# Low parts of the keys made by POOL from a ScalarE copy, from the third head pair on

## The chip, the core and the metric

The kernel runs on one core of one Trainium2 chip. The metric is the device time of one execution in microseconds; lower is better. Engines are named as the profile names them: PE is TensorE, DVE is VectorE, ACT is ScalarE, POOL is GpSimd, SP issues most of the DMAs.

## The reference

One layer of a streaming encoder, batch 1, 1024 positions, model width 1024. A modulated layer norm feeds one input projection; eight heads of forgetting attention and eight of stick-breaking attention, each 64 wide, read its columns; each head's output is gated by a SiLU, and all go through one output projection into a residual and a last layer norm.

```python
u = _layer_norm(x) * (1.0 + scale) + shift
h = u @ w_in[layer]
fq, fk, fv, fg, ff, sq, sk, sv, sg = _split_columns(h)
...
# forgetting attention, per head and block of 128 queries
s = einsum('bhqd,bhkd->bhqk', q, k) * scale + (f_q[..., :, None] - f_k[..., None, :])
p = softmax(where(causal, s, -inf)); out = p @ v
...
# stick-breaking attention
z = einsum('bhqd,bhkd->bhqk', q, k) * scale
later = cumsum(log_sigmoid(-z), reverse=True) - log_sigmoid(-z)   # on the strict causal part
w = where(strict, exp(log_sigmoid(z) + later), 0); out = w @ v
...
y = concatenate([y_fox * silu(fg), y_sb * silu(sg)]) @ w_out[layer]
x = _layer_norm(alpha * x + gate * y, ln_g, ln_b)
```

## The kernel before

Products are made more exact by splitting operands into a rounded high part and a low part (the remainder) and adding several matmuls: a projection takes three matmuls for each block of 128 of the contraction (`L255`, `L256`, `L257`: high input by high weight, low by high, high by low). The weights are split by POOL: `L124` makes the high part, `L125` the low part (`L826`, `L827` do the same for the attention output read back from memory).

The sixteen heads are worked as eight pairs; a pair fills 128 partitions, head 0 in rows 0 to 63 and head 1 in rows 64 to 127. Pairs 0 to 3 are stick-breaking, 4 to 7 forgetting attention. One unit of attention is a pair, a head and a block of 128 queries. A unit's scores go into one PSUM tile `S` of 1024 columns, of which there is one buffer: `L410` multiplies keys by the queries' high and low parts, `L411` the low parts of the keys (`klo`, traced as `kl`) by the queries (`qz`, copied by ACT at `L388`). In stick-breaking units ACT reads `S` twice (`L430` into `kp`, `L431` into `be`), DVE scans `kp` (`L436`, `L440`), POOL multiplies (`L444`). In forgetting units DVE takes the row sums (`L417` into `a` and `nm`), ACT the exponential (`L423`), DVE the reciprocal, POOL the scaling (`L425`). Two units later PE transposes the weights into `T` (`L461`, two PSUM buffers), ACT copies the high part to `pt` (`L463`), DVE makes its low part (`L464`), and after every second unit PE multiplies by the values (`L476`) into `pv`. ACT copies half of `pv` into a `ty` tile (`L495`, two SBUF buffers), DVE adds (`L496`), POOL applies the gate (`L497`), and SP stores it to memory (`L505`, traced as `y_dr<-ty`).

The projections of the next pairs (`gen_m`; values by `v_tile`, `L310` to `L312`) are filled in between the matmuls of attention. Each half of 512 positions is accumulated in a PSUM tile of the tag `acc`, which has two buffers, and evicted by `evac_m`: for keys that is `evac_k`. There ACT rounds each head's rows into `kst` (`L240`, traced as `k<-m`), SP copies the rounded rows to the other half of the partitions (`L242`), and DVE subtracts the rounded values from the accumulator into `klo` (`L243`). The accumulator's buffer is free for a later projection when both subtractions are done.

PE's order is written out by hand; the orders of ACT, DVE, POOL and SP are set by a scheduler when the kernel is built, by its own estimates.

Of the kernel before, what the change touches and what calls it, by code (L numbers as in the profile page):

```python
# [8 lines left out]
F32 = mybir.dt.float32  # L9
F32R = mybir.dt.float32r  # L10
AF = mybir.ActivationFunctionType
ALU = mybir.AluOpType

P = 128
# [4 lines left out]
HD = 64  # L19
# [8 lines left out]
def tile_hybrid_layer(  # L28
# [17 lines left out]
    nc = tc.nc  # L46

    cp = ctx.enter_context(tc.tile_pool(name="const", bufs=1))
    sb = ctx.enter_context(tc.tile_pool(name="sb", bufs=1))
# [185 lines left out]
    def evac_k(p, ch, acc, kst, klo, heads):  # L235
        s = slice(ch * 512, ch * 512 + 512)
        for h in heads:
            r = slice(h * HD, h * HD + HD)
            o = slice((1 - h) * HD, (1 - h) * HD + HD)
            first = nc.scalar.copy(kst[h][r, s], acc[r, :])  # L240
            kf = kst[h].bitcast(F32)
            nc.sync.dma_start(kf[o, s], kf[r, s])  # L242
            last = nc.vector.tensor_tensor(klo[r, s], acc[r, :], kf[r, s], op=ALU.subtract)  # L243
        return first, last

    def evac_g(p, ch, acc, sg):
# [12 lines left out]
    qst, kst, klo, sgt, vt = {}, {}, {}, {}, {}  # L259
# [11 lines left out]
    def evac_m(p, m, ch, acc, heads=(0, 1)):  # L271
        if m == 0:
            evac_q(p, ch, acc, qst[p], heads)
        elif m == 1:
            return evac_k(p, ch, acc, kst[p], klo[p], heads)
        else:
            evac_g(p, ch, acc, sgt[p])
# [364 lines left out]
    for kb in range(NB):  # L642
        last = kb == NB - 1
# [95 lines left out]
    for kb in range(NB):  # L739
# [13 lines left out]
        if kb < len(evacs):  # L753
            n, h = evacs[kb]
# [209 lines left out]
    for k in range(len(units) + LAG + 1):  # L964
        if k < len(units):
# [12 lines left out]
            p, h, i = units[k]  # L978
# [86 lines left out]
```

## Time and profile before

| what | value |
|---|---|
| median of 3 runs (lowest, highest) | 690.2 us (690.01, 690.37) |
| the profiled execution's own time | 689.96 us |
| its span in the profile | 688.2 us |
| busy: PE, DVE, ACT, POOL | 98%, 66%, 56%, 62% |
| granted TensorE clock, mean | 0.998 |

The span is what the records cover; the rest of an execution's time lies around it. Rows of a group read: line, engine, operation, output and inputs, shape and count, then busy time and mean nanoseconds of one, then the idle time ahead of them and what ended it. Rows of a timeline read: start in us, duration in us, engine, line and operation; in brackets the idle time ahead and what ended it. A row with x2 stands for two like operations in a row.

### The profile page before, as it was taken

Reading aid. Unit: us, or ns where it says so; the run is one execution under the profiler, and the core shown is the slowest. Engines: PE = TensorE matmul, PEld = TensorE weight load, DVE = VectorE, ACT = ScalarE, POOL = GpSimd, SP = SyncE. Lnnn points to the kernel's source line nnn. Section 1 sums busy time; section 2 is a strip of 40 time slices with the busy share of each in tenths; the row PEclk is TensorE's granted clock in tenths of the full one; section 3 lists DMA queues with packets and bytes.
Section 4 is the critical chain, followed back from the end, with each engine's and each line's share of the span. In section 5 each row is a group of like instructions: output and inputs, shape, how many; then the busy total and the mean of one; then the engine's idle time right before and its main releaser. Section 6 shows DMA issues by size and latency. Waiting matters only on the chain.

```text
span 688.2 us, 11786 instructions
## 1 busy us (share of the span) xinstructions
PE 674.0 (98%) x4033; PEld 589.7 (86%) x4033; DVE 453.5 (66%) x924; ACT 382.1 (56%) x862; POOL 425.7 (62%) x555
## 2 busy tenths in 40 slices
PE   8999999999999999999999999999999999999996
PEld 4789898888998888889998888889988889888885
DVE  5985458767657676767675665656665767774645
ACT  5666457856657666666674564655565666531000
POOL 4567978656439565556388897877584364665411
PEclk9999999999999999999999999999999999999999
DMA  8956232112102122112144553454341288143301
GB/s 306 416 233 230 85 108 57 26 40 53 40 9 70 41 55 55 38 47 62 25 136 153 177 160 116 146 163 145 100 143 46 67 293 352 56 155 119 128 32 61
DMA packets 44028, 81.59 MB, mean 119 GB/s; under 512 B 5120, under 2 KB 18752, under 8 KB 43072
## 3 DMA queue, kind: packets, MB, share of 16 engines
q1 hardware_dynamic: 42816, 76.65, 34.0%
q10 hardware_dynamic: 1152, 4.19, 2.2%
q8 instruction: 32, 0.52, 0.3%
q14 instruction: 28, 0.23, 0.1%
HBM read 60.34 MB, written 16.29 MB: 111 GB/s over the span
## 4 chain that ended last, share of the span: by engine, by line
PE 92%; DVE 3%; DMA 2%; POOL 1%; issue 1%; ACT 0%; SPq 0%; POOLq 0%; DVEq 0%
PE m L255 10%; PE pv L476 10%; PE m L256 10%; PE m L257 10%; PE T L461 9%; PE S L411 5%; PE S L410 5%; PE o L848 4%; PE o L846 4%; PE o L847 4%; PE v L310 4%; PE v L312 4%; PE v L311 4%; DMA wss<-in_w_ss_dram 1%; DMA x<-in_x_dram 1%
## 5 line engine op out<-in xcount | busy, mean ns | idle before, releaser
L255 PE MATMUL m<-uh,whi 128*128 128x512 f32 x304 | 126.4, 416 | 0.5 <-DVE kl L243 0.5
L256 PE MATMUL m<-ul,whi 128*128 128x512 f32 x304 | 119.8, 394 | 0.0
L257 PE MATMUL m<-uh,wlo 128*128 128x512 f32 x304 | 119.6, 394 | 0.0
L464 DVE TENSOR_TENSOR pt<-T,pt 128x512 fp32r<-128x512 f32 (+2 forms) x192 | 100.5, 550 | 17.9 <-ACT pt L463 16.8
L444 POOL TENSOR_TENSOR be<-be,kp 128x127 f32<-128x127 f32 (+3 forms) x64 | 77.1, 1205 | 33.5 <-DVE kp L440 23.6
L463 ACT CAST pt<-T 128x512 fp32r<-128x512 f32 (+2 forms) x192 | 85.7, 480 | 16.7 <-PE T L461 13.0
L436 DVE TENSOR_TENSOR_SCAN kp<-kp,floor 128x512 f32<-128x512 f32 (+2 forms) x64 | 65.1, 1018 | 32.1 <-ACT kp L430 31.3
L476 PEld LDWEIGHTS pv<-pt,v 128*128 128x128 f32 (+1 forms) x640 | 77.2, 163 | 4.5 <-DVE pt L464 0.7
L476 PE MATMUL pv<-pt,v 128*128 128x256 f32 (+3 forms) x640 | 80.5, 271 | 0.5 <-DVE pt L464 0.5
L425 POOL TENSOR_SCALAR a<-a,l 128x1024 f32<-128x1024 f32 (+3 forms) x64 | 47.9, 748 | 39.5 <-DVE l L424 25.9
L423 ACT ACTIVATE a<-a,nm 128x1024 f32<-128x1024 f32 (+3 forms) x64 | 49.8, 778 | 34.0 <-DVE nm L417 33.0
L257 PEld LDWEIGHTS m<-uh,wlo 128*128 128x128 f32 x304 | 57.1, 188 | 13.5
L410 PE MATMUL S<-k,q 128*128 128x512 f32 (+5 forms) x192 | 66.5, 348 | 0.2 <-DVE nm L417 0.2
L411 PE MATMUL S<-kl,qz 128*128 128x512 f32 (+5 forms) x192 | 65.5, 342 | 0.0
L255 PEld LDWEIGHTS m<-uh,whi 128*128 128x128 f32 x304 | 57.3, 188 | 9.2 <-DVE kl L243 0.9
L256 PEld LDWEIGHTS m<-ul,whi 128*128 128x128 f32 x304 | 57.4, 189 | 8.0
L497 POOL TENSOR_TENSOR ty<-ty,sg 64x256 f32<-64x256 f32 x64 | 47.4, 741 | 24.6 <-DVE ty L496 12.2
L417 DVE CUSTOM_DVE_ANT_0 a<-S,fb 128x1024 f32<-128x1024 f32 (+3 forms) x64 | 48.3, 755 | 20.4 <-PE S L411 9.8
L430 ACT ACTIVATE kp<-S 128x128 f32<-128x128 f32 (+3 forms) x64 | 41.7, 651 | 31.8 <-PE S L411 28.3
L310 PE MATMUL v<-whi_v,uh 128*128 128x256 f32 (+1 forms) x192 | 56.0, 292 | 0.7 <-DVE kl L243 0.7
L388 ACT CAST qz<-q 64x128 fp32r<-64x128 f32 x128 | 37.4, 295 | 33.0 <-PE S L411 31.9
L312 PE MATMUL v<-wlo_v,uh 128*128 128x256 f32 (+1 forms) x192 | 54.2, 282 | 0.0
(291 smaller groups left out, 1611.5 us busy)
## 6 DMA issues: line engine op xcount, KB each, us to landing
raw<-in_w_qkg_dram SPq DMA_DIRECT2D x38, 256.0 KB, 2.8
wss<-in_w_ss_dram SPq DMA_DIRECT2D x7, 1024.0 KB, 8.3
x<-in_x_dram SPq DMA_DIRECT2D x8, 512.0 KB, 7.3
k<-k SPq DMA_DIRECT2D x32, 128.0 KB, 2.5
wg<-in_w_gate_dram SPq DMA_DIRECT2D x8, 512.0 KB, 4.4
raw_o<-in_w_out_dram SPq DMA_DIRECT2D x16, 256.0 KB, 2.7
fb<-f_dr ACTq DMA_DIRECT2D x8, 512.0 KB, 4.2
wo_dr<-whi_o SPq DMA_DIRECT2D x16, 256.0 KB, 2.5
```

The costliest lines, as they stand in the source:

```text
L255: nc.tensor.matmul(acc, hi[:, c], u_hi[kt][:, s], start=(kt == 0), stop=False)
L256: nc.tensor.matmul(acc, hi[:, c], u_lo[kt][:, s], start=False, stop=False)
L257: nc.tensor.matmul(acc, lo[:, c], u_hi[kt][:, s], start=False, stop=(kt == NB - 1))
L310: nc.tensor.matmul(acc[:, :n], u_hi[kt][:, ts_], hi[:, s], start=(kt == 0), stop=False)
L312: nc.tensor.matmul(acc[:, :n], u_hi[kt][:, ts_], lo[:, s], start=False, stop=(kt == NB - 1))
L410: nc.tensor.matmul(S[:, s, :w], qst[p][h][:, qs], kst[p][h][:, ks], start=True, stop=False)
L411: nc.tensor.matmul(S[:, s, :w], z, klo[p][:, ks], start=False, stop=True)
L436: scan = nc.vector.tensor_tensor_scan(rv, rv, floor[0][:, 512 - n:][:, ::-1], initial=0.0, op0=ALU.mult, op1=ALU.max)
L444: nc.gpsimd.tensor_tensor(be[:, :ke - 1], be[:, :ke - 1], kp[:, 1:ke], op=ALU.mult)
L463: nc.scalar.copy(hi[:, :n, qo:qo + P], t3)
L464: nc.vector.tensor_tensor(lo[:, :n, qo:qo + P], t3, hi.bitcast(F32)[:, :n, qo:qo + P], op=ALU.subtract)
L476: nc.tensor.matmul(acc[:m, q0:256], vt[p][:, kb, h * P:h * P + m], pt[:, kb % 4, q0:], start=start, stop=stop)
```

## The change

For pairs 2 to 7, in both halves, ACT copies the whole accumulator (128 by 512, unrounded) into an SBUF tile of the tag `ty` after the two casts, and POOL subtracts the rounded keys from that copy, one head's 64 rows at a time. DVE no longer takes part, and only ACT reads the accumulator. Pairs 0 and 1 stay as they were. Lines behind the edit move down by 7 in the changed kernel: its copy is `L247`, its subtraction `L250`, and a line such as `L425` is `L432` there.

```diff
             first = nc.scalar.copy(kst[h][r, s], acc[r, :])
             kf = kst[h].bitcast(F32)
             nc.sync.dma_start(kf[o, s], kf[r, s])
-            last = nc.vector.tensor_tensor(klo[r, s], acc[r, :], kf[r, s], op=ALU.subtract)
+            if p < 2:
+                last = nc.vector.tensor_tensor(klo[r, s], acc[r, :], kf[r, s], op=ALU.subtract)
+        if p >= 2:
+            whole = sb.tile([P, 512], F32, tag="ty", bufs=2, name=f"kr_{p}_{ch}")
+            nc.scalar.copy(whole, acc)
+            for h in heads:
+                r = slice(h * HD, h * HD + HD)
+                last = nc.gpsimd.tensor_tensor(klo[r, s], whole[r, :], kst[h].bitcast(F32)[r, s], op=ALU.subtract)
         return first, last
```

PE's order is the same on both sides. The scheduler gives the others new orders. ACT around the second half of pair 3's keys, while attention works on pair 2, head 1 (`kp_1_3` is head 1, block 3, with the pair left out; the number at the end of a name is a buffer), before:

```order
L463 CAST pt_2_1_0_0_3062<-T_1_0_0_3064 128x128
L240 CAST k_0_2893<-m_1_1_2996 64x512
L430 ACTIVATE kp_1_3_3083<-S_1_3_3080 128x512
L431 ACTIVATE be_1_3_3084<-S_1_3_3080 128x512
L388 CAST qz_83<-q_1_1577 64x128
L463 CAST pt_2_1_0_0_3062<-T_1_1_0_3103 128x2x128
L240 CAST k_1_2894<-m_1_1_2996 64x512
L430 ACTIVATE kp_1_4_3121<-S_1_4_3116 128x640
```

and in the changed kernel:

```order
L470 CAST pt_2_1_0_0_3068<-T_1_0_0_3070 128x128
L240 CAST k_0_2897<-m_1_1_3002 64x512
L240 CAST k_1_2898<-m_1_1_3002 64x512
L247 COPY kr_1_3084<-m_1_1_3002 128x512
L437 ACTIVATE kp_1_3_3091<-S_1_3_3088 128x512
L438 ACTIVATE be_1_3_3092<-S_1_3_3088 128x512
L395 CAST qz_83<-q_1_1577 64x128
L470 CAST pt_2_1_0_0_3068<-T_1_1_0_3111 128x2x128
```

The second cast has moved ahead of the reads of `S`, and the copy stands behind it. DVE around the second half of pair 6's keys, before:

```order
L243 TENSOR_TENSOR kl_5332<-m_1_1_5437,k_0_5330 64x512
L464 TENSOR_TENSOR pt_5_0_1_0_5472<-T_0_2_0_5518,pt_5_0_1_0_5471 128x3x128
L417 ISA a_1_7_5553,nm_1_7_5554<-S_1_7_5548,fb_5063 128x1024
L417 ISA nm_1_7_5554 128x1
L243 TENSOR_TENSOR kl_5332<-m_1_1_5437,k_1_5331 64x512
L395 TENSOR_TENSOR fb_5063<-fb_5063,ps_causal 128x128
```

and in the changed kernel:

```order
L431 RECIPROCAL l_0_0_5509<-l_0_0_5509 128x1
L424 ISA a_1_7_5573,nm_1_7_5574<-S_1_7_5568,fb_5079 128x1024
L424 ISA nm_1_7_5574 128x1
L471 TENSOR_TENSOR pt_5_0_1_0_5490<-T_0_2_0_5538,pt_5_0_1_0_5489 128x3x128
L402 TENSOR_TENSOR fb_5079<-fb_5079,ps_causal 128x128
```

Both subtractions are gone, and the row sums now stand ahead of the low part of `pt`. POOL around the second half of pair 7's keys, before:

```order
L826 TENSOR_SCALAR whi_y_4_6893<-yr_4_6891 128x384
L827 TENSOR_TENSOR wlo_y_4_6894<-yr_4_6891,whi_y_4_6893 128x384
L826 TENSOR_SCALAR whi_y_0_7199<-yr_0_7197 128x512
L827 TENSOR_TENSOR wlo_y_0_7200<-yr_0_7197,whi_y_0_7199 128x512
L425 TENSOR_SCALAR a_1_1_6749<-a_1_1_6749,l_1_1_6751 128x256
```

and in the changed kernel:

```order
L834 TENSOR_TENSOR wlo_y_4_6918<-yr_4_6915,whi_y_4_6917 128x384
L833 TENSOR_SCALAR whi_y_0_7223<-yr_0_7221 128x512
L250 TENSOR_TENSOR kl_6561<-kr_1_6766,k_0_6559 64x512
L250 TENSOR_TENSOR kl_6561<-kr_1_6766,k_1_6560 64x512
L834 TENSOR_TENSOR wlo_y_0_7224<-yr_0_7221,whi_y_0_7223 128x512
L432 TENSOR_SCALAR a_1_1_6773<-a_1_1_6773,l_1_1_6775 128x256
```

The two subtractions stand ahead of a weight split's second half and of the scaling of `a`.

## The prediction

> **What bounds the kernel now.** I read the page's busy shares and the chain that ended last, then the waits of TensorE, then the groups by shape of the operations that the diff touches, then the timeline of each engine around each of the twelve places where a 512-key half is evicted. The page first:
>
> ```profile
> PE 674.0 (98%) x4033; PEld 589.7 (86%) x4033; DVE 453.5 (66%) x924; ACT 382.1 (56%) x862; POOL 425.7 (62%) x555
> PE 92%; DVE 3%; DMA 2%; POOL 1%; issue 1%; ACT 0%; SPq 0%; POOLq 0%; DVEq 0%
> ```
>
> TensorE is the bound. Its matmuls are the same in kind, number and order on both sides of the diff, so the time can move only by what TensorE waits. The two waits that the edited lines cause, of all its waits:
>
> ```profile
> PE v L310 <- DVE kl L243: 0.7, 1, 0.7
> PE m L255 <- DVE kl L243: 0.5, 1, 0.5
> ```
>
> Each is one event: a new accumulation that needs the PSUM buffer which the last L243 of a key half still reads. The other 22 L243 release it in time. So at most these two can be won, and every loss must come from TensorE waiting for something made late by the added work. Relieving VectorE as such is worth nothing at 66% busy.
>
> **The change, part by part.** The prices:
>
> ```profile
> L243 DVE TENSOR_TENSOR kl<-m,k 64x512 fp32r<-64x512 f32 x24 | 16.5, 687 | 8.1 <-ACT k L240 7.8
> L240 ACT CAST k<-m 64x512 fp32r<-64x512 f32 x24 | 13.9, 581 | 9.5 <-PE m L257 9.0 <-DVE kl L243 0.3
> L125 POOL TENSOR_TENSOR wlo<-raw,whi 128x512 fp32r<-128x512 f32 x38 | 49.1, 1294 | 3.1 <-DMA wo_dr<-wlo_o 1.5
> L497 POOL TENSOR_TENSOR ty<-ty,sg 64x256 f32<-64x256 f32 x64 | 47.4, 741 | 24.6 <-DVE ty L496 12.2 <-issue 6.7 <-PE v L311 1.7
> ```
>
> VectorE loses 24 x 0.687 = 16.5 us. ScalarE gains 12 copies of 128x512 from PSUM. Its 64x512 cast takes 0.581 and a 128x512 activation from PSUM 0.59 (under L1), so I take 0.59 each, 7 us in all. POOL gains 24 subtractions of 64x512, a shape it does not run before. Its 64x256 product takes 741 ns and its 128x512 subtraction 1294: twice the elements per row cost 1.75 times, whatever the rows. So I take 1.29 for a 64-row one, 2.58 a half, 31 us in all; the floor is half of that, if the two halves of the partitions ran at once. On average both engines have room (56% and 62%); what counts is each place.
>
> At each place ScalarE now runs cast, cast, copy back to back, where before the second cast stood some operations later. What stood between is delayed by a cast and a copy, and what stood behind the old second cast by the copy alone.
>
> *Gain G1, second half of pair 2.*
>
> ```profile
> 171.57 0.58 ACT L240 CAST k<-m 64x512 fp32r<-64x512 f32 x1 [0.75 <-PE m L257]
> 174.64 0.58 ACT L240 CAST k<-m 64x512 fp32r<-64x512 f32 x1
> 176.19 0.69 DVE L243 TENSOR_TENSOR kl<-m,k 64x512 fp32r<-64x512 f32 x1
> 175.93 0.27 PE L411 MATMUL S<-kl,qz 128*128 128x128 f32 x1
> 176.94 0.39 PE L310 MATMUL v<-whi_v,uh 128*128 128x264 f32 x1 [0.74 <-DVE kl L243]
> ```
>
> The second cast stood behind 3 us of score work and VectorE's subtraction behind two scans. With the casts at 171.57 and some 0.49 apart (step shown under L1) the copy ends near 173.15, so the buffer is free 3 us before it is asked for. What TensorE loses lies between 0.74, the idle time by the modelled end of L411, and 176.94 - 175.93 = 1.01, start to start: 0.9 gained.
>
> *Gain G2, second half of pair 7.*
>
> ```profile
> 552.12 0.58 ACT L240 CAST k<-m 64x512 fp32r<-64x512 f32 x1
> 552.80 0.39 PE L256 MATMUL m<-ul,whi 128*128 128x512 f32 x1
> 553.03 0.39 PE L257 MATMUL m<-uh,wlo 128*128 128x512 f32 x1
> 553.90 0.50 PE L255 MATMUL m<-uh,whi 128*128 128x512 f32 x1 [0.48 <-DVE kl L243]
> ```
>
> The step of these matmuls is 0.23, so 553.90 would be 553.26: 0.64 gained, as the copy ends near 552.1.
>
> *Loss L1, second half of pair 3.*
>
> ```profile
> 262.25 0.58 ACT L240 CAST k<-m 64x512 fp32r<-64x512 f32 x1 [0.85 <-PE m L257]
> 262.73 0.59 ACT L430 ACTIVATE kp<-S 128x512 f32<-128x512 f32 x1
> 263.22 0.59 ACT L431 ACTIVATE be<-S 128x512 f32<-128x512 f32 x1
> 264.13 0.31 PE L410 MATMUL S<-k,q 128*128 128x320 f32 x1
> ```
>
> ScalarE starts 512-wide operations 0.49 apart. L430 and L431 read the only score buffer in PSUM; L410 writes it next. L431 ends at 263.81, 0.32 ahead of L410. With a cast and a copy put ahead, 2 x 0.49 = 0.98 later, it ends at 264.79: TensorE waits 0.7.
>
> *Losses L2, L3, second halves of pairs 4 and 6.* Here the copies of transposed weights are pushed back.
>
> ```profile
> 314.98 0.85 ACT L463 CAST pt<-T 128x512 fp32r<-128x512 f32 x2
> 315.88 1.00 DVE L464 TENSOR_TENSOR pt<-T,pt 128x512 fp32r<-128x512 f32 x2
> 316.60 1.49 PE L476 MATMUL pv<-pt,v 128*128 128x256 f32 x12
> 458.57 0.47 ACT L463 CAST pt<-T 128x384 fp32r<-128x384 f32 x1
> 459.77 1.21 DVE L417 CUSTOM_DVE_ANT_0 a<-S,fb 128x1024 f32<-128x1024 f32 x1
> 460.56 1.00 PE L476 MATMUL pv<-pt,v 128*128 128x256 f32 x8
> ```
>
> Pair 4: the second L463 ends 315.83, then 316.81; its low part on VectorE (0.5 to 0.7) ends near 317.4 to 317.5, and the products on low parts begin after some seven of the twelve: 316.60 + 7 x 1.49/12 = 317.47. I take 0.2. Pair 6: L463 moves to 459.55 to 460.02; VectorE now does the 1.21 us L417 first (it can start near 459.4, to 460.65), so the low part ends near 461.15 where the third product, 460.56 + 0.3, wants it: 0.3.
>
> *Loss L4, second half of pair 7, on POOL.* In the new order both subtractions stand between the two halves of a split, ahead of L425.
>
> ```profile
> 552.90 0.62 POOL L826 TENSOR_SCALAR whi_y<-yr 128x512 fp32r<-128x512 f32 x1
> 553.60 1.28 POOL L827 TENSOR_TENSOR wlo_y<-yr,whi_y 128x512 fp32r<-128x512 f32 x1
> 554.86 0.49 POOL L425 TENSOR_SCALAR a<-a,l 128x256 f32<-128x256 f32 x1
> 557.11 0.39 PE L411 MATMUL S<-kl,qz 128*128 128x512 f32 x1
> 558.17 0.38 PE L461 MATMUL T<-ident,a 128*128 128x128 f32 x2
> ```
>
> Three 1.26 steps from 553.60 put L425 at 557.38 to 557.87; the transpose that reads it, 0.64 earlier by G2, asks at 557.53. That waits 0.35, or 0.65 if the first half's subtractions have made POOL 0.3 late: 0.5. The low parts themselves end at 556.12, in time for L411 at 556.47. Most of G2 is thus given back.
>
> The Trainium skill (GPSIMD Engine Reference, section 2.1) says that a POOL core serves its own 16 partitions and goes on to the next instruction as soon as its own share is done; the two 64-row subtractions would then run side by side. By that rule a half costs 1.29 and L4 is gone; the sum would be 0.5 lower. No row of this profile shows it. Against it here: the new program makes the second subtraction wait on POOL's own semaphore.
>
> *Buffers.* The copy takes one of the two ty buffers, so the next ty copy waits for the store of the ty before it. The tightest place is pair 5:
>
> ```profile
> 399.57 0.45 SPq L505 DMA_DIRECT2D y_dr<-ty  x1
> 400.94 0.37 ACT L495 COPY ty<-pv 64x256 f32<-64x256 f32 x1 [0.70 <-issue]
> 403.81 0.30 ACT L388 CAST qz<-q 64x128 fp32r<-64x128 f32 x1 [1.40 <-PE S L411]
> 402.36 1.29 POOL L125 TENSOR_TENSOR wlo_o<-raw_o,whi_o 128x512 fp32r<-128x512 f32 x1
> 406.01 0.95 ACT L463 CAST pt<-T 128x512 fp32r<-128x512 f32 x2
> 407.56 1.97 PE L476 MATMUL pv<-pt,v 128*128 128x256 f32 x16
> y_dr<-ty SPq DMA_DIRECT2D x56, 64.0 KB, 1.9
> 396.00:410.00 14.00, 14.00 (x87) 12.38 (x85) 9.55 (x23) 9.16 (x22) 13.71 (x15) 1.00 0.55 168
> ```
>
> The store lands near 399.57 + 1.9 = 401.5 where L495 stood at 400.94: ScalarE stalls 0.5, under its idle 1.40 before 403.81. In the second half L463's pair ends at 406.96, then 407.94, and the second tile's first product comes some three steps into 407.56: 0.1 taken. In the other places the score and weight reads stand further off than the 0.98 by which they move, and I cost them at nothing; the cover is TensorE's own queue of matmuls. SP's queue: the second cast's DMA goes out earlier, and y stores that wait for POOL up to 2.6 us later, with the weight loads behind them; those are asked for several microseconds ahead: nothing, unless POOL's lag adds up (rival B).
>
> Sum: 0.9 + 0.64 - 0.7 - 0.2 - 0.3 - 0.5 - 0.1 = -0.26 us, a loss. The profiled execution took 689.96, 0.24 under the median of 690.2 and 1.8 over its span of 688.2. 689.96 + 0.26 = 690.2 for such an execution, and 690.5 for the median.
>
> **Rivals.** *A, faster:* both waits go and the pushed work stays under TensorE's queue. 690.2 - 1.54 = 688.7. For it: two waits with names; against it: L1, where one row's slack of 0.32 stands against two added operations.
>
> *B, slower:* the third ScalarE operation waits for POOL. The copy of pair 5's second half takes the buffer that the first half's subtractions read. In the window of 14 us POOL is busy 13.71 already; by my count the subtractions end at 403.65 + 2.58 = 406.23 (they follow 402.36's low-part split) and the copy stands at 406.53, so 0.3 to spare. If POOL is one half's worth, 2.58, later, ScalarE stands 2.3 with pt behind it, and the products at 407.56 wait about as long: 690.5 + 2.3 = 692.8. It decides for slower from some 1.4 us late on, one 512-wide POOL operation more than I count. For it: the 13.71; against it: the new order moves L425 ahead of splits, so that what TensorE waits for goes first.
>
> *C:* the subtractions overlap, as under L4: 690.0. *D:* nothing on TensorE's path moves, gains included, because the accumulator's next user is set otherwise: 690.2, told from the forecast by rows alone.
>
> **How the numbers follow.** A change of this kernel can be told from none at about 0.2%, 1.4 us. The forecast 0.45, A 0.16, B 0.27, C and D 0.12 together. The likeliest is 690.5, its own range 689.3 to 691.7, as L1 to L4 each may be off by their own half and place. Faster (under 688.8) holds most of A, 0.15; slower (over 691.6) B and the upper edge of the forecast, 0.29; the rest, 0.56, is the same. The range runs from A's 688.7 to B's 692.8.
>
> **What would show it.** The two waits on kl gone from TensorE's list; a wait of L410 on L431's be near 264 of 0.7; a wait of T on POOL's a near 557 of 0.5; small waits of L476 on pt near 317 and 461. POOL's new group: 24 at about 1.29. Wrong if POOL's mean is near 0.65 or over 1.5, if the copy takes far more than 0.59, or if ScalarE's ty group idles long on POOL or a DMA.

## The result and the profile after

| | before | changed |
|---|---|---|
| median of 9 runs | 690.2 us | 692.23 us |
| ratio of the runs (95% interval) | | 1.0031 (1.0021 to 1.0041) |
| profiled execution, its span | 689.96, 688.2 us | 692.39, 690.7 us |

The changed kernel is slower by 2.0 us, 0.3%. The page's line of busy times after, and TensorE's list of waits:

```profile
PE 674.7 (98%) x4033; PEld 589.5 (85%) x4033; DVE 438.4 (63%) x900; ACT 388.6 (56%) x874; POOL 455.7 (66%) x579
```

```profile
PE xT_early L212 <- ACT x L198: 1.1, 2, 0.9
...
PE S L417 <- ACT be L438: 0.8, 1, 0.8
PE pv L483 <- DVE pt L471: 0.5, 1, 0.5
PE T L468 <- POOL a L432: 0.5, 1, 0.5
PE S L418 <- POOL kl L250: 0.4, 1, 0.4
```

One line of the same list before:

```profile
PE pv L476 <- DVE pt L464: 0.5, 1, 0.5
```

The groups of the moved work, after:

```profile
L250 POOL TENSOR_TENSOR kl<-kr,k 64x512 fp32r<-64x512 f32 x24 | 30.9, 1286 | 7.7 <-ACT kr L247 6.8
L247 ACT COPY kr<-m 128x512 f32<-128x512 f32 x12 | 7.0, 587 | 0.3
L240 ACT CAST k<-m 64x512 fp32r<-64x512 f32 x24 | 13.9, 580 | 9.3 <-PE m L264 9.0
```

Both waits on VectorE's kl are gone from TensorE's list. In their place stand two that were named ahead of the run (scores on `be`, transposes on POOL's `a`) and one that was not: the scores on POOL's `kl`. The products' wait on `pt` is no new one: it stands in the list before with the same 0.5, at 116 us, where nothing is edited. The small waits of products that the forecast named near 317 and 461 are too short for the list; they show in the start times below. The wait on `x` at the top is at the start of the kernel. Both new groups cost what they were priced at, 1.286 and 0.587 us. The idle time of `L247`, 0.3 us in all twelve, says that the copy hardly ever waits for its buffer.

TensorE does the same 4033 matmuls in the same order on both sides. So each can be paired with itself, and the difference of its two start times, after less before, shows where time is lost: it stays level and moves in steps. In the table a place's value is the difference behind it less that ahead of it; minus is a gain. "Again" is a second profile of the changed kernel, "alone" a kernel with the change in that pair only (experiments below).

| place (time before) | forecast | after | again | alone |
|---|---|---|---|---|
| start, up to 30 us | 0 | +0.58 | +0.32 | -0.06 to +0.37 |
| G1, pair 2, second half (177) | -0.90 | -0.97 | -0.97 | -0.97 |
| L1, pair 3, second half (264) | +0.70 | +1.08 | +1.08 | +1.08 |
| L2, pair 4, second half (317) | +0.20 | +0.47 | +0.46 | |
| pair 5, second half (407) | +0.10 | +0.28 | +0.31 | |
| L3, pair 6, second half (460) | +0.30 | +0.25 | +0.25 | |
| G2, pair 7, second half (553) | -0.64 | -0.72 | -0.72 | -0.73 |
| L4, pair 7 (557 and 558) | +0.50 | +1.44 | +1.44 | +1.21 |
| the rest | 0 | +0.03 | +0.02 | |
| end of the span | +0.26 | +2.44 | +2.19 | |

The time went to few places. The seven edited ones were all named ahead, and their losses are mostly larger than forecast. They come to +1.83; nearly all that is left is the start. There no edited line runs, and TensorE waits for the first rows of x (ScalarE's first work on them before, after, and in the second profile of the changed kernel):

```profile
7.92 1.24 ACT L198 ACTIVATE x<-x,rs_a 128x1024 f32<-128x1024 f32 x1 [5.06 <-POOL rs_a L191]
```

```profile
8.78 1.24 ACT L198 ACTIVATE x<-x,rs_a 128x1024 f32<-128x1024 f32 x1 [5.94 <-POOL rs_a L191]
```

```profile
7.58 1.24 ACT L198 ACTIVATE x<-x,rs_a 128x1024 f32<-128x1024 f32 x1 [4.94 <-POOL rs_a L191]
```

In the second profile the first rows came early and the second rows late (11.14, against 9.70 before and 11.06 after). In all three the orders of TensorE, VectorE, ScalarE and POOL are the same up to 163 us.

### The profile page after: what moved, and what is told of

Read it like the earlier page. It is cut to its first block, busy times and chain, and to the rows that moved or that the text cites. A ratio compares the mean times of both kernels' runs of the same rounds, so it can differ in the third digit from the quotient of the medians.

```text
span 690.7 us, 11801 instructions
## 1 busy us (share of the span) xinstructions
PE 674.7 (98%) x4033; PEld 589.5 (85%) x4033; DVE 438.4 (63%) x900; ACT 388.6 (56%) x874; POOL 455.7 (66%) x579
## 4 chain that ended last, share of the span: by engine, by line
PE 52%; DVE 1%; POOL 1%; issue 0%; POOLq 0%; ACT 0%
PE pv L483 6%; PE T L468 5%; PE m L262 5%; PE m L263 5%; PE m L264 5%; PE o L855 4%; PE o L853 4%; PE o L854 4%; PE S L418 3%; PE S L417 3%; PE v L317 2%; PE v L319 2%; PE v L318 2%; DVE a L424 0%; POOL wlo_y L834 0%
## 5 line engine op out<-in xcount | busy, mean ns | idle before, releaser
L432 POOL TENSOR_SCALAR a<-a,l 128x1024 f32<-128x1024 f32 (+3 forms) x64 | 47.9, 748 | 34.7 <-DVE l L431 23.9
```

## The experiments

**The changed kernel again, and one pair at a time.** The edits set the condition under which a pair is evicted by the copy; all else is as before the change. The condition of the subtraction from the accumulator is its opposite.

```diff
-        if p >= 2:      # and the subtraction from the accumulator for p < 2
+        if p == 2:      # kernels only2, only3, only7: p == 2, p == 3, p == 7
```

> The changed kernel once more, unedited. Theory S (sites): the time is the sum of what TensorE gains and loses at the seven places read from the trace of after: -0.90, +0.95, +0.24, +0.21, +0.24, -0.64, and +0.59 and +0.68 in pair 7, together +1.37; the +0.5 that the start lost in that profile (before 20 us, where no edited line runs) is a matter of the run. So the seven steps come back within 0.1 us each and the start may differ; time 691.6 to 692.3. Theory G (general load): the extra time goes with the amount of work added to ScalarE and POOL, spread over the kernel; the steps come back too, but so does the 0.5 of the start, in every profile: 692.2.

> The change for pair 2 alone; the other pairs as before. S: only the gain of the second half of pair 2 is left, 690.2 - 0.9 = 689.3, and no wait of TensorE on kl near 176. G: a sixth of the added work, 690.2 + 2.0/6 = 690.5.

> The change for pair 3 alone. S: 690.2 + 0.95 = 691.15, with one wait of the scores on the second reading of S by ScalarE near 264. G: 690.5.

> The change for pair 7 alone. S: 690.2 - 0.64 + 0.59 + 0.68 = 690.8: the wait on kl near 553 goes, and two waits on POOL near 557 and 558 come. G: 690.5. The rival of the prediction in which only the waits go: 689.6.

| kernel | median, before in the same session | change |
|---|---|---|
| again | 692.19, 690.01 | +2.18, ratio 1.0035 (1.0022 to 1.0047) |
| pair 2 alone | 689.38, 690.01 | -0.63, ratio 0.9989 (0.9980 to 0.9997) |
| pair 3 alone | 691.45, 690.01 | +1.44, ratio 1.0020 (1.0011 to 1.0028) |
| pair 7 alone | 690.37, 690.01 | +0.36, ratio 1.0005 (0.9997 to 1.0014) |

The places behave as separate terms: each pair alone gives its own steps and none elsewhere behind the start of over 0.2 us (the table above), and the general-load theory falls, since pair 2 alone gains, while its sixth of the work was to cost 0.3. G1 and L1 come back to 0.01 us. Pair 7's loss is smaller alone, 1.21 against 1.44. The pairs ahead do not show as its cause. With TensorE's own lag taken off, POOL's last gate product of pair 6 and the reload that hangs on it (both in the next experiment) start at the same time in the two kernels, to 0.02 us, but with pair 7 alone the reload's data are used 0.2 us sooner. Why that transfer is faster is open. The start is not settled. In the profiles it is between -0.06 and +0.58 later than in the one profile of before, and the medians of the kernels with pair 2 and pair 3 alone are 0.3 and 0.4 above what their places give. The two profiles of the changed kernel differ by 0.26 there, so a shift of that size comes without any edit.

**The first half of pair 7 as before.** I looked at POOL and SP around pair 7, before (in the first fence the gate product and SP's store and reload, in the second the same after):

```profile
545.84 0.74 POOL L497 TENSOR_TENSOR ty<-ty,sg 64x256 f32<-64x256 f32 x1 [1.49 <-issue]
...
546.60 0.46 SPq L505 DMA_DIRECT2D y_dr<-ty  x1
548.54 0.91 SPq L823 DMA_DIRECT2D yr<-y_dr  x2
...
551.33 0.51 POOL L826 TENSOR_SCALAR whi_y<-yr 128x384 fp32r<-128x384 f32 x1 [1.71 <-DMA yr<-y_dr]
```

```profile
544.97 2.64 POOL L250 TENSOR_TENSOR kl<-kr,k 64x512 fp32r<-64x512 f32 x2 [2.14 <-ACT kr L247]
547.71 0.69 POOL L432 TENSOR_SCALAR a<-a,l 128x512 f32<-128x512 f32 x1
548.48 0.74 POOL L504 TENSOR_TENSOR ty<-ty,sg 64x256 f32<-64x256 f32 x1
...
549.25 0.46 SPq L512 DMA_DIRECT2D y_dr<-ty  x1
551.19 0.92 SPq L830 DMA_DIRECT2D yr<-y_dr  x2
...
554.02 0.51 POOL L833 TENSOR_SCALAR whi_y<-yr 128x384 fp32r<-128x384 f32 x1 [2.60 <-PE pv L483]
...
556.18 2.65 POOL L250 TENSOR_TENSOR kl<-kr,k 64x512 fp32r<-64x512 f32 x2
558.91 1.31 POOL L834 TENSOR_TENSOR wlo_y<-yr,whi_y 128x512 fp32r<-128x512 f32 x1
560.20 0.48 POOL L432 TENSOR_SCALAR a<-a,l 128x256 f32<-128x256 f32 x1
...
558.89 0.50 PE L418 MATMUL S<-kl,qz 128*128 128x512 f32 x1 [0.43 <-POOL kl L250]
560.74 0.44 PE L468 MATMUL T<-ident,a 128*128 128x128 f32 x2 [0.52 <-POOL a L432]
```

The gate product moved by 2.64 (545.84 to 548.48). TensorE itself stands 1.9 later here; the other 0.7 is that the two subtractions of the first half, and a scaling of `a`, now stand ahead of it. The store, the reload and the split `whi_y` (of the attention output, not of weights) follow, the last by 2.69 (551.33 to 554.02), so POOL has fallen back by 0.8 against TensorE. The second half's subtractions stand behind that split. (The releaser named at 554.02 is not the cause: the reload issued at 551.19 is what the split reads, and it took 2.7 us to arrive.) The theory was that this push makes half of L4.

```diff
-        if p >= 2:
+        if p >= 2 and (p, ch) != (7, 0):
```

> As the changed kernel, but the first half of pair 7 is evicted as before (VectorE, from the accumulator). Theory: POOL's two subtractions of that first half push pair 6's last gate product back by 0.9, with it the store, the load of y and the splits of y, and so the second half's subtractions; without them the low parts end near 557.9 on the clock of after and the scores wait no more (0.59 gone), the transpose waits 0.35 instead of 0.68: 692.2 - 0.9 = 691.3. Rival: the order on POOL in the second half alone makes both waits: 692.2, with both waits as they were.

691.14 against 689.97: ratio 1.0016 (1.0007 to 1.0025), 1.05 less than the changed kernel, where 0.9 was expected. In its profile the wait of the scores is gone and L4 is 0.60; only the transpose's wait stays, at 0.36:

```profile
547.41 0.74 POOL L504 TENSOR_TENSOR ty<-ty,sg 64x256 f32<-64x256 f32 x1 [1.47 <-issue]
...
552.86 0.51 POOL L833 TENSOR_SCALAR whi_y<-yr 128x384 fp32r<-128x384 f32 x1 [1.67 <-DMA yr<-y_dr]
...
559.56 0.44 PE L468 MATMUL T<-ident,a 128*128 128x128 f32 x2 [0.36 <-POOL a L432]
```

TensorE stands 1.58 later than before here, and the gate product and the split are later by 1.57 and 1.53: the push is gone. So of L4's 1.44 the first half of pair 7 makes 0.84, by a push through POOL, a store, a reload and a split to the second half.

**VectorE subtracts from the copy.**

```diff
-                last = nc.gpsimd.tensor_tensor(klo[r, s], whole[r, :], kst[h].bitcast(F32)[r, s], op=ALU.subtract)
+                last = nc.vector.tensor_tensor(klo[r, s], whole[r, :], kst[h].bitcast(F32)[r, s], op=ALU.subtract)
```

> As the changed kernel, but VectorE makes the low parts from the copy, not POOL, in pairs 2 to 7. ScalarE's order and its copies are the same. S: the two waits on POOL in pair 7 go (0.59 + 0.68) and the ScalarE losses stay (0.95 + 0.24 + 0.21 + 0.24) with both gains (0.90 + 0.64): +0.1, so 690.3, or 690.8 if the start loses 0.5. G with POOL's load as the cause: 690.2 or less, and the ScalarE losses gone as well. If the copy in the ty buffers were the cause: as the changed kernel, 692.2.

706.78 against 689.97, ratio 1.0228 (1.0207 to 1.0249): far from any of the three. POOL's waits in pair 7 did go, but TensorE loses 6.8 at pair 4, 5.0 at pair 5 and 4.5 at pair 6, and at pair 2 it gives back 1.3 behind G1. The group, and VectorE, POOL and TensorE at pair 4:

```profile
L250 DVE TENSOR_TENSOR kl<-kr,k 64x512 fp32r<-64x512 f32 x24 | 27.2, 1133 | 12.9 <-ACT kr L247 12.6
```

```profile
317.99 4.43 DVE L250 TENSOR_TENSOR kl<-kr,k 64x512 fp32r<-64x512 f32 x2 [1.01 <-ACT kr L247]
322.46 1.02 DVE L471 TENSOR_TENSOR pt<-T,pt 128x512 fp32r<-128x512 f32 x2
...
317.97 1.99 POOL L451 TENSOR_TENSOR be<-be,kp 128x1023 f32<-128x1023 f32 x1
319.93 1.25 POOL L125 TENSOR_TENSOR wlo<-raw,whi 128x512 fp32r<-128x512 f32 x1
...
323.20 1.65 PE L483 MATMUL pv<-pt,v 128*64 128x256 f32 x7 [3.90 <-DVE pt L471]
```

The subtraction that takes 0.687 from the accumulator takes 1.13 on average from the copy, and this pair of them 4.43: it ends only after two POOL instructions that run back to back. The twelve that met no POOL instruction but a memset took 0.68 or 0.69; of the other twelve, eleven took 0.84 to 4.01. The theory formed then: with both inputs in SBUF, VectorE's subtraction is held while POOL works.

The waits are not all of the loss. Behind them TensorE ran at a lower granted clock (the third figure from the end of the row; ahead of it stand the busy times of the five engines):

```profile
323.00:328.50 5.50, 5.29 (x26) 5.30 (x27) 2.38 (x6) 1.43 (x3) 2.36 (x3) 0.50 0.09 27
```

The clock was 0.50 from 321.6 to 328.5 and in two stretches of 3.4 us at pairs 5 and 6; the other kernels' profiles have it at 1.00 from 10 us to the last 7 us. Products of 0.28 us took 0.41 in these stretches, which makes some 5.5 of the 16 us lost at pairs 4 to 6. The five runs agree: 703.6 and 704.6 with a mean clock of 0.995 and 0.994, 706.8 to 707.8 with 0.989.

**VectorE subtracts from the accumulator, the copy made all the same.** This kernel has the orders of the last one; only where one operand lies differs.

```diff
-                last = nc.vector.tensor_tensor(klo[r, s], whole[r, :], ...
+                last = nc.vector.tensor_tensor(klo[r, s], acc[r, :], ...
```

> As the kernel with VectorE's subtraction from the copy, but VectorE reads the accumulator in PSUM again; ScalarE still makes the copy, which nobody reads. Both kernels have the same orders on every engine, so only the place of one operand differs. Theory P (two SBUF operands): VectorE's subtraction of two SBUF operands is held while POOL works through back-to-back instructions, one with a PSUM operand is not; all 24 take 0.69 and the long ones (up to 4 us) go; what remains are ScalarE's losses and both gains: -0.97 + 1.08 + 0.47 + 0.28 + 0.25 - 0.72 = +0.4, with 0.3 of the start 690.7. Rival O (order): it is the place of the subtractions on VectorE that makes the transposed weights late; 705 or so, as before.

The group on VectorE, and two of TensorE's waits:

```profile
L250 DVE TENSOR_TENSOR kl<-m,k 64x512 fp32r<-64x512 f32 x24 | 16.5, 688 | 12.4 <-ACT kr L247 12.1
```

```profile
PE m L262 <- DVE kl L250: 0.5, 1, 0.5
PE pv L483 <- DVE pt L471: 3.6, 4, 1.5
```

694.31 against 690.09, ratio 1.0061 (1.0048 to 1.0075). All 24 take 0.68 or 0.69, so the place of the operand is what held them; it is worth 12.5 of the 706.78, with the stretches at a clock of 0.50, which are gone too. But 690.7 was expected, and both theories hold a part: with both subtractions together ahead of the low parts of `pt`, pair 4 loses 1.41 in place of 0.47, pair 5 1.15 in place of 0.28, pair 6 1.70 in place of 0.25, and G2's wait on kl is back. The two subtractions stand behind the cast and ahead of work that TensorE needs sooner. In the changed kernel POOL keeps these 1.4 us off VectorE. Against this kernel the move to POOL is worth some 2 us (694.3 and 692.2); the kernel before, whose subtractions stand elsewhere in VectorE's order, is faster than either.

The Trainium skill (SBUF — State Buffer, section "SBUF: two separate sides") says that VectorE with two SBUF inputs and a GpSimd operation that reads SBUF share a port pair as an exclusive lock for the whole instruction. The trace agrees, 0.69 with a PSUM operand against up to 4.01, and adds that VectorE may wait through two POOL instructions in a row (317.97 to 321.18), not one.

**The order of the casts.** Pair 3 alone lost 1.08 where 0.7 was forecast. ScalarE after, and the scores:

```profile
261.89 1.19 ACT L240 CAST k<-m 64x512 fp32r<-64x512 f32 x2 [0.81 <-PE m L264]
263.10 0.59 ACT L247 COPY kr<-m 128x512 f32<-128x512 f32 x1
263.58 0.60 ACT L437 ACTIVATE kp<-S 128x512 f32<-128x512 f32 x1
264.07 0.60 ACT L438 ACTIVATE be<-S 128x512 f32<-128x512 f32 x1
...
264.73 0.42 PE L417 MATMUL S<-k,q 128*128 128x320 f32 x1 [0.79 <-ACT be L438]
```

From the first cast to the copy are 1.21 us, two steps of 0.605, not of the 0.49 forecast; behind the copy the steps are 0.48 and 0.49. The second cast works on rows 64 to 127. The matmul behind the wait, too, takes 0.42 where it took 0.31 before, and the next starts 0.11 later for it.

```diff
-        for h in heads:
+        for h in (heads[::-1] if p == 3 else heads):
```

> The change for pair 3 alone, with the cast of head 1 (rows 64 to 127) ahead of that of head 0; ScalarE's order is else that of the kernel with pair 3 alone. Theory: ScalarE starts the next operation 0.48 after a 512-wide one when both begin at row 0, and 0.605 when either begins at row 64; then the steps are 0.605, 0.48, 0.48, the scores' operations come 0.12 earlier, and the loss near 264 is 0.96 instead of 1.08: 691.3. Rival: casts that read the same accumulator never overlap: steps 0.605, 0.605, 0.48 and the loss 1.08 as it was, 691.45.

ScalarE at the same place in this kernel:

```profile
262.47 1.19 ACT L240 CAST k<-m 64x512 fp32r<-64x512 f32 x2 [0.81 <-PE m L264]
263.56 0.58 ACT L247 COPY kr<-m 128x512 f32<-128x512 f32 x1
264.04 0.59 ACT L437 ACTIVATE kp<-S 128x512 f32<-128x512 f32 x1
264.52 0.59 ACT L438 ACTIVATE be<-S 128x512 f32<-128x512 f32 x1
```

From the first cast to the copy are now 1.09, that is 0.61 and 0.48: the cast of rows 0 to 63, now the second, overlaps the copy behind it. The place's loss is 0.94 in place of 1.08, as expected. The median, 691.32 against 690.09, ratio 1.0018 (1.0009 to 1.0027), can't be told from pair 3 alone; the verdict rests on the steps.

**The copy only where the profile of before has a wait.**

```diff
+        if (p, ch) in ((2, 1), (7, 1)):   # all other halves as before
             whole = sb.tile(...); nc.scalar.copy(whole, acc)
             ...                            # pair 2: POOL subtracts, pair 7: VectorE
```

> The copy only where the profile of before has a wait on kl: second half of pair 2 (POOL subtracts) and second half of pair 7 (VectorE subtracts from the copy); everything else as before. S: -0.90 - 0.64 = -1.54, 688.7, faster than both kernels. Rival: something else takes the place of the waits: ScalarE's casts and copy in pair 7 delay the next weights' copies, or VectorE's subtractions, now later than before, the low parts that the scores read: 689.3 or more.

688.56 against 689.97, ratio 0.9979 (0.9970 to 0.9988): faster than both kernels. Its profile has G1's -0.97 and G2's -0.73 and no step of over 0.1 in between. Neither kl wait is left on TensorE's list. VectorE's two subtractions in pair 7 take 0.98 and 1.0, beside POOL's split, and nobody waits for them.

## Why the prediction was right and wrong

The measured 692.2 lies in the range of 688.7 to 692.8, but the likeliest time was 690.5 and its own range ended at 691.7; the case "slower" had 0.29. A loss of 0.3 was forecast and 2.0 came. That the range holds it is luck in part: its upper end came from rival B, which did not happen. What follows is by the prediction's terms.

- *That only TensorE's waits count, and that relieving VectorE is worth nothing.* Right: 15 us less of VectorE's busy time (453.5 to 438.4) brought nothing beside the two waits.
- *The prices.* Right: 1.286 against 1.29 for the subtraction, 0.587 against 0.59 for the copy.
- *G1 and G2.* Right: -0.97 and -0.72 against -0.90 and -0.64.
- *L1, and with it L2 and pair 5.* The mechanism was right (ScalarE's reads and copies pushed back by a cast and a copy), the size was not: 1.08, 0.47 and 0.28 against 0.7, 0.2 and 0.1. The step that failed is "some 0.49 apart" for all three ScalarE operations. It was read from operations that begin at row 0; the steps into and out of the second cast are 0.605. Work behind the copy moves by 1.21 in place of 0.98, which is 0.23 of the difference; turning the casts round took 0.14 of L1 off again. Another 0.11 of L1 is the slower first matmul behind the wait, which no term had. At pairs 4 and 5 the place was not quite the one named: most of the loss (0.34 of 0.47, and nearly all of 0.28) stands at the first product, whose high part ScalarE now copies too late, and not at the later products of the forecast. At pair 4 the first of the two copies ends at 317.53:

```profile
316.93 0.87 ACT L470 CAST pt<-T 128x512 fp32r<-128x512 f32 x2
317.58 1.71 PE L483 MATMUL pv<-pt,v 128*128 128x256 f32 x12
```

- *L3.* Right in size and place, 0.25 against 0.3, at the third product.
- *L4.* The step that failed is "0.3 late" for what the first half's subtractions do to POOL. It was 0.8, because they stand ahead of pair 6's last gate product, and a store, a reload and a split hang on it. So the low parts were late for L411, called "in time", by 0.6, and the transpose waited longer: 1.44 against 0.5. Undoing the first half alone took 0.84 of it away. The 0.60 that stayed is still over the 0.35 forecast for a POOL on time. A part of this is that the three steps of 1.26 were 4.01 in that kernel and not 3.78: a subtraction that waits for the one ahead starts 1.35 behind it.
- *The buffers and rival B.* B fell, though the time came out on its side: the copy waits 0.3 in all for its buffer. What I costed at nothing there, a y store that POOL delays, did cost, but in pair 7 (under L4) and not in pair 5.
- *Rival A* fell: the waits go, but the pushed work shows. *Rival C* fell: 2.64 and 2.65 for two subtractions, one behind the other. The rule of the Trainium skill (GPSIMD Engine Reference, section 2.1) that a core goes on alone does not show in this program, whose second subtraction waits on POOL.
- *The start.* A change of 0.3 to 0.6 there was no term. Whether the edit causes any of it is open.

## What to carry to other kernels

Where the bound engine is 98% busy, cost a change by place: list its waits, and for each edited place the slack of what is pushed; three kernels with the change in one pair each showed that such terms add up, to some 0.2 us. Follow a pushed instruction past its own engine: what it delays here reached the bound engine through a store and a reload ten microseconds on. If only two of twelve places wait, change only those two: that, with VectorE subtracting at one of them, gave -1.4 us where all twelve gave +2.0.

## What the runs showed of the hardware

- VectorE's subtraction of two SBUF operands took 0.68 to 4.01 us, depending on what POOL ran; with one operand in PSUM all 24 took 0.68 or 0.69.
- ScalarE started a 128x512 copy 0.48 us after a 64x512 cast of rows 0 to 63, but 0.605 after one of rows 64 to 127 (all twelve halves of the changed kernel, 0.604 to 0.609). From one of the two casts to the other it was 0.60 to 0.61 (once 0.585), whichever rows came first.
- POOL took 1.286 us for a subtraction of 64 rows by 512, and 1.294 for one of 128 rows; two of 64 rows, the second waiting for the first, took 2.64.
- In the kernel in which VectorE subtracts from the copy, TensorE's waits at pairs 4, 5 and 6 (one of 3.9, two of 1.0 and one of 2.8 us) came with stretches of 6.8, 3.4 and 3.4 us at a granted clock of 0.50. A single wait of 1.1 us at pair 2, and the longest of 1.5 in the kernel with the accumulator, came with none.
